# Second modulation product of a diffusion step: one 2 MB weight transfer and one buffer per group

## The chip, the cores and the metric

The kernel runs on one core of one Trainium2 chip. The metric is device time in microseconds, smaller is better. The kernel before takes 1057.17 us (median of 3 runs, 1056.76 to 1060.57).

## What is computed

One layer of a hybrid diffusion backbone, for 512 latent and 128 context tokens (640 rows of 1024 features), all in float32. Cut to the part that matters here:

```python
shift1, scale1, gate1, shift2, scale2, gate2 = jnp.split(silu(c) @ w_ada + b_ada, 6)   # for c and for c_ctx
h   = rmsnorm(x, pre1) * (1 + scale1) + shift1
mix = (g_a * y_mlstm + g_b * y_attn) @ w_out          # two mixers that both read h; g = sigmoid of h @ w_in
x   = x + gate1 * rmsnorm(mix, post1)
h   = rmsnorm(x, pre2) * (1 + scale2) + shift2
x   = x + gate2 * rmsnorm(square(relu(h @ w_mlp1)) @ w_mlp2, post2)
```

`w_ada` is 1024 x 6144. The product with it has two rows only (the latent condition `c` and the context condition `c_ctx`). Its first 2048 columns (shift1, scale1) are needed at the start; the other 4096 (scale2, shift2, gate1, gate2) are the "second modulation product", and the change is there.

## The kernel before

Large products run on TensorE in three matmuls each, on a high and a low part of the operands: `mm3` (L115) issues them on L116, L117 and L118, and names like `wh`/`wl`, `h1h`/`h1l` are such pairs. Weights reach SBUF as `raw` by SyncE's DMA queue (`load_w`, L103); ScalarE casts the high part (L111), VectorE subtracts for the low part (L112). `raw` has two buffers, and three pairs of `wh`/`wl` go round as a ring.

The stage around the change is the merge of the two mixers, from 352 to 553 us of the span. A loop over eight column blocks `j` does, for each: a product for the gate of the first mixer (48 matmuls of 320 columns), one with that mixer's output (24), the same two for the second mixer (48 and 24), then sigmoid, multiply and add on ScalarE and VectorE (L805, L808, L810) and the split of the sum into `zh`, `zl` (L811, L812). The next stage, the product with `w_out`, reads `zh` and `zl`.

The second modulation product is spread over this loop. It is a generator, `ada_rest` (L737), with eight groups `cb` of 512 columns; one step is taken ahead of the loop (L795) and one at the end of each turn (L813). A group

- loads its weights, 1024 x 512 floats or 2 MB, from GpSimd's DMA queue: four transfers of 512 KB, two k-blocks each, into a tile `aw2` with two buffers (L741, L742; the profile writes `aw` for it, as for the tile of the first product);
- multiplies in `ada_rows` (L144): eight float32 matmuls of 512 columns (L149), one per k-block. Each has a stationary operand of 32 columns (`csil`, the two conditions padded with zeros) and is put on one of four strips of the array, 32 columns wide, by `tile_position`: k-blocks 0 to 3 on strips 0 to 3, then 4 to 7 on the same strips again, added up there. In the profile each float32 matmul counts as two instructions;
- copies the result from PSUM (L150, ScalarE, tile `ar`), turns it by four transposes on TensorE (L155), adds the strips and the bias on VectorE (L157, L158), and writes it to `modA`, `modB` or `gcol`; every second of the last four groups also sends a gate to DRAM (L759 to L762).

The first product (w_ada1, in `features`, L198) uses the same `ada_rows`, with 256 columns and its weights in one 1 MB transfer per feature block from SyncE's queue.

The program is put in order by a scheduler that works from modelled times (`schedule_with_timeline_sim`): each engine runs its own list strictly in that order, and waits on semaphores. With two buffers for four transfers, the third and the fourth pair of matmuls of a group can only run after the first and second buffers have been read and filled again, so the scheduler puts them further down TensorE's list.

Of the kernel before, what the change touches and what calls it, by code (L numbers as in the profile page):

```python
# [6 lines left out]
F32 = mybir.dt.float32  # L7
# [5 lines left out]
P = 128  # L13
NT = 5
TOK = 640
KD = 8
# [10 lines left out]
def _build(ctx, tc, nc, a, dbg):  # L27
    V, S, G, T = nc.vector, nc.scalar, nc.gpsimd, nc.tensor
# [46 lines left out]
    def bank1():  # L75
        return psum[1][1].tile([P, 512], F32, name="b1")
# [67 lines left out]
    def ada_rows(raws, n, rows):  # L144

        ps = bank1()
        for k in range(KD):
            j = k % 4
            T.matmul(ps[32 * j:32 * j + 32, 0:n], csil[:, k, :], raws[k], start=k < 4, stop=k >= 4, tile_position=(0, 32 * j))  # L149
        S.copy(rows, ps[:, 0:n])  # L150

    def ada_cols(rows, nb, pt, cb, name):

        for fb in range(nb):
            T.transpose(pt[:, fb, :], rows[:, fb * 128:(fb + 1) * 128], ident)  # L155
        m = small.tile([P, 4, 2], F32, name="mc" + name)[:, 0:nb, :]
        V.tensor_reduce(out=m, in_=pt.rearrange("p b (j x) -> p b x j", j=4)[:, :, 0:2, :], axis=AX.X, op=ALU.add)  # L157
        V.tensor_tensor(out=m, in0=m, in1=b_ada[:, cb:cb + nb].unsqueeze(2).broadcast_to([P, nb, 2]), op=ALU.add)  # L158
        return m
# [89 lines left out]
    with pool("pM", side="right") as pM:  # L249
# [68 lines left out]
        for s in (4, 0, 1, 2, 3):  # L318
            c = slice(s * 128, (s + 1) * 128)
            V.tensor_tensor_scan(out=mt[:, c], data0=ar[:, c], data1=ar[:, c], initial=mc[:, s:s + 1], op0=ALU.max, op1=ALU.max)  # L320
            if s != 3:
                d = 5 if s == 4 else s + 1
# [17 lines left out]
        for (dst, src) in ((Rr, R), (srr, sr)):  # L340
            n = dst.shape[0]
# [394 lines left out]

    def ada_rest(pY):  # L737
        for cb in range(8):
            raws = []
            for u in range(4):  # L740
                raw = pY.tile([P, 2, 512], F32, name="aw2", bufs=2)  # L741
                G.dma_start(raw, a["w_ada2"][cb * 4 + u].rearrange("p (k n) -> p k n", k=2))  # L742
                raws += [raw[:, 0, :], raw[:, 1, :]]
            rows = pY.tile([P, 512], F32, name="ar2", bufs=1)
            ada_rows(raws, 512, rows)
            m = ada_cols(rows, 4, bank1().rearrange("p (b x) -> p b x", b=4), 16 + cb * 4, "2")
            kk = slice((cb % 2) * 4, (cb % 2) * 4 + 4)
            if cb < 2:
                V.scalar_tensor_tensor(out=modA[1][:, kk, :], in0=m, scalar=1.0, in1=pre2[:, kk].unsqueeze(2).broadcast_to([P, 4, 2]),
                                       op0=ALU.add, op1=ALU.mult)  # L750
            elif cb < 4:
                V.tensor_copy(modB[1][:, kk, :], m)
            else:
                g = (cb - 4) // 2
                V.tensor_tensor(out=gcol[g][:, :, kk].rearrange("p r k -> p k r"), in0=m,
                                in1=post[:, g, kk].unsqueeze(2).broadcast_to([P, 4, 2]), op=ALU.mult)
                if cb % 2:
                    pg = bank1()
                    T.transpose(pg[0:16, 0:128], gcol[g].rearrange("p r k -> p (r k)"), ident)  # L759
                    gr = pY.tile([16, 128], F32, name="gr", bufs=1)  # L760
                    V.tensor_copy(gr, pg[0:16, 0:128])
                    G.dma_start(a["scratch_gate"][g].rearrange("r (k f) -> (r k) f", f=128), gr)  # L762
            yield
# [6 lines left out]
    with pool("pY", side="right") as pY:  # L770
        ys = []
        ada = ada_rest(pY)
        for name in ("m", "a"):
            yh = pY.tile([P, 4, TOK], F32R, name="yh" + name)
# [263 lines left out]
    def u_pair():  # L1038
        return [[pF_.tile([P, TOK], F32R, name="u" + s, bufs=4) for n in range(2)] for s in "hl"]

    for ch in range(NCH):
# [25 lines left out]
        else:  # L1067
# [9 lines left out]
            for p in range(2):  # L1077
                n = ch * 2 + p
# [4 lines left out]
                u = u_pair()  # L1083
# [34 lines left out]
        for j, (t, nh, i, lo, hi) in enumerate(todo):  # L1118
            d = slice(nh * 512 + lo, nh * 512 + hi)
# [15 lines left out]
            if last and hi == 512 and nh:  # L1135
                r = small.tile([P, 1], F32, name="rs_y")
                G.tensor_tensor(out=r, in0=ms, in1=mhalf[:, 0:1], op=ALU.pow)
                for h in range(2):
                    d = slice(h * 512, h * 512 + 512)
# [14 lines left out]
def _piece_b(w):  # L1154
    import numpy as np
    kk, n = w.shape[0] // 128, w.shape[1] // 128
    return np.ascontiguousarray(w.reshape(kk, 128, n, 128).transpose(2, 1, 0, 3).reshape(n, 128, kk * 128))


def _piece_a(w, k, n):  # L1160
    import numpy as np
    nk, nn = w.shape[0] // (128 * k), w.shape[1] // n
    return np.ascontiguousarray(w.reshape(nk, k, 128, nn, n).transpose(3, 0, 2, 1, 4).reshape(nn * nk, 128, k * n))


def prepare(i):
    import numpy as np
    c_ = np.ascontiguousarray
    cols = lambda v: c_(v.reshape(-1, 128).T)
    d = {}  # L1170
    d["x"] = c_(np.concatenate([i["x_sample"][0], i["x_prompt"][0]], 0).reshape(5, 128, 1024))
    d["cache_ckv"] = c_(i["cache_mla_ckv"][0, 0])
    d["cache_krope"] = c_(i["cache_mla_krope"][0, 0])
    cn = i["state_mlstm_C"][0, 0].transpose(0, 2, 1, 3)
    nn = i["state_mlstm_n"][0, 0].transpose(0, 2, 1)[..., None]
    d["state"] = c_(np.concatenate([cn, nn], -1))
    cv = np.stack([i["c_ctx"], i["c"][0]], -1)
    cv = cv.reshape(8, 128, 2).transpose(1, 0, 2).reshape(128, 16)
    wa = i["w_ada"][0].reshape(1024, 6, 8, 128)
    d["w_ada1"] = _piece_a(wa[:, [1, 0]].transpose(0, 2, 1, 3).reshape(1024, 2048), 8, 256)  # L1180
    d["w_ada2"] = _piece_a(wa[:, [4, 3, 2, 5]].reshape(1024, 4096), 2, 512)
    b = i["b_ada"][0].reshape(6, 8, 128)
    b = np.concatenate([b[[1, 0]].transpose(1, 0, 2).reshape(16, 128), b[[4, 3, 2, 5]].reshape(32, 128)], 0).reshape(-1)
    d["vecs"] = c_(np.concatenate([cols(i["norm_pre1"][0]), cols(i["norm_pre2"][0]), c_(i["mlstm_head_norm"][0].T), cols(b),
                                   cols(i["norm_post1"][0]), cols(i["norm_post2"][0]), cv], 1))
    gb = i["mlstm_gate_b"][0]
    d["hvec"] = c_(np.stack([gb[:, 0].reshape(8), gb[:, 1].reshape(8), i["state_mlstm_m"][0, 0].reshape(8)], 1))
    d["kv_norm"], d["q_norm"] = c_(i["mla_kv_norm"][0]), c_(i["mla_q_norm"][0])
    w = i["w_in"][0]
    d["w_q"], d["w_k"] = _piece_b(w[:, 0:512]), _piece_b(w[:, 512:1024])  # L1190
    d["w_v"], d["w_o"] = _piece_a(w[:, 1024:1536], 2, 512), _piece_b(w[:, 1536:2048])
    d["w_p1"] = _piece_a(np.concatenate([w[:, 2048:2064], w[:, 2448:2704], w[:, 2704:2736]], 1), 2, 304)
    d["w_cq"] = _piece_a(w[:, 2064:2448], 2, 384)
    d["w_g"] = _piece_b(w[:, 2736:4784])
    d["w_uq"] = _piece_a(i["w_uq"][0].reshape(384, 768), 1, 768)
    ukv = i["w_ukv"][0]
    d["w_uk"] = c_(_piece_b(ukv[:, :, 0:64].reshape(256, 512)).transpose(1, 0, 2).reshape(128, 1024))
    d["w_uv"] = _piece_a(ukv[:, :, 64:128].reshape(256, 512), 2, 512)[0]
    d["w_y"] = c_(np.concatenate([_piece_b(i["w_mlstm_o"][0]), _piece_b(i["w_mla_o"][0])], 2))
    d["w_out"] = _piece_a(i["w_out"][0], 2, 512)  # L1200
    d["w_mlp1"] = _piece_b(i["w_mlp1"][0])
    d["w_mlp2"] = c_(i["w_mlp2"][0].reshape(8, 2, 2, 128, 2, 512).transpose(0, 4, 1, 3, 2, 5).reshape(8, 2, 2, 128, 1024))
    d = {k: c_(np.asarray(v)) for k, v in d.items()}

    f = np.float32
    eye = np.eye(128, dtype=f)
    s, t = np.arange(128)[:, None], np.arange(128)[None, :]
    pen_f = np.where(t >= s, 0.0, BIG).astype(f)
    pen_b = np.where(t <= s, 0.0, BIG).astype(f)
    inv = (f(10000.0) ** (-np.arange(0, 16, 2, dtype=f) / f(16))).astype(f)  # L1210
    pos = np.arange(512)
    ang = np.concatenate([(pos // 64).astype(f)[:, None] * inv, (pos % 64).astype(f)[:, None] * inv], -1)
    tab = lambda x: x.astype(f).reshape(4, 128, 16).transpose(1, 0, 2).reshape(128, 64)
    d["consts"] = c_(np.concatenate([eye, eye[::-1], pen_f, pen_b, tab(np.cos(ang)), tab(np.sin(ang))], 1))
    keep = np.ones((8, 640), f)
    keep[:, ::128] = 0.0
    d["keep"] = keep
    return d
# [28 lines left out]
```

## Time and profile before

| | |
|---|---|
| median of 3 runs | 1057.17 us (1056.76 to 1060.57) |
| the profiled execution | 1055.42 us, of which 1053.7 us is the span from first to last instruction |
| mean granted TensorE clock | 0.996 of full |
| TensorE busy | 1022.7 us, 97% of the span |
| VectorE, ScalarE, GpSimd busy | 53%, 40%, 23% |
| bytes moved by DMA | 112.03 MB, 106 GB/s on average |

The span is what the profile's rows add up to; 1.7 us lie around it. The profiled execution is 1.75 us below the median of the runs. Busy times on TensorE are of pipelined matmuls, whose ends are modelled, so the steps from one start to the next say more than the durations.

### The profile page before, as it was taken

To read this page: it belongs to the slowest core of one execution; us is meant where nothing else is said; L and a number is where in the kernel's file an instruction comes from. 1 tells how busy PE (TensorE), PEld (TensorE's weight loads), DVE (VectorE), ACT (ScalarE), POOL (GpSimd) and SP (SyncE) were. 2 spreads that over 40 slices of the span, in tenths; PEclk is the share of its full clock that TensorE was granted. 3 is DMA by queue.
4 is the path that set the end of the run, shared out by engine and by line. 5 is a ranking of instruction groups with operands and counts; after the bars stand their busy time and mean duration, and the time that the engine had idled before them with its cause. 6 is when DMAs were issued, how large, how long until landed. Compare 5 with 4: busy or idle time off the path is not lost.

```text
span 1053.7 us, 15728 instructions
## 1 busy us (share of the span) xinstructions
PE 1022.7 (97%) x6342; PEld 907.0 (86%) x6342; DVE 561.0 (53%) x955; ACT 424.2 (40%) x784; POOL 238.1 (23%) x218
## 2 busy tenths in 40 slices
PE   4999999899999999999999998999999999999997
PEld 2899899888889888888888897898989898989896
DVE  4655255767664222222334489365566565656557
ACT  4354244277775222222223564442425152515142
POOL 3011225424560000001000015224040404040101
PEclk9999999999999999999999999999999999999999
DMA  9444132211002444444446251231313131313034
GB/s 372 168 129 145 46 109 73 75 41 41 15 8 79 139 143 140 141 140 141 140 141 223 77 180 62 79 121 40 120 40 120 40 120 41 121 41 121 1 111 169
DMA packets 40121, 112.03 MB, mean 106 GB/s; under 512 B 4280, under 2 KB 14168, under 8 KB 38768
## 3 DMA queue, kind: packets, MB, share of 16 engines
q1 hardware_dynamic: 34656, 92.92, 25.8%
q0 software_dynamic: 4672, 16.80, 4.9%
q10 hardware_dynamic: 720, 1.31, 0.3%
q8 instruction: 50, 0.82, 0.3%
q14 instruction: 23, 0.19, 0.1%
HBM read 105.03 MB, written 5.98 MB: 105 GB/s over the span
## 4 chain that ended last, share of the span: by engine, by line
PE 89%; DVE 5%; ACT 2%; issue 2%; DMA 1%; POOL 1%; SPq 0%; POOLq 0%; DVEq 0%; ACTq 0%
PE b L116 20%; PE b L117 20%; PE b L118 20%; PE b L937 7%; PE bY L937 5%; PE b L149 3%; PE bV L937 2%; PE bW L937 2%; PE b L695 2%; PE b L683 2%; PE b L229 1%; PE b L496 1%; PE b L470 1%; DMA x<-x 1%; DMA gate<-w_mlp 1%
## 5 line engine op out<-in xcount | busy, mean ns | idle before, releaser
L112 DVE TENSOR_TENSOR wl<-raw,wh 128x1024 fp32r<-128x1024 f32 (+2 forms) x67 | 80.5, 1202 | 157.7 <-ACT wh L111 156.4
L111 ACT CAST wh<-raw 128x1024 fp32r<-128x1024 f32 (+2 forms) x69 | 69.8, 1013 | 175.0 <-PE b L117 157.0
L117 PE MATMUL b<-h1l,wh 128*128 128x320 f32 x400 | 125.2, 313 | 0.0
L116 PE MATMUL b<-h1h,wh 128*128 128x320 f32 x384 | 119.9, 312 | 0.0
L118 PE MATMUL b<-h1h,wl 128*128 128x320 f32 x384 | 118.9, 310 | 0.0
L117 PEld LDWEIGHTS b<-h1l,wh 128*128 128x128 f32 x400 | 75.2, 188 | 6.9 <-issue 6.9
L116 PEld LDWEIGHTS b<-h1h,wh 128*128 128x128 f32 x384 | 72.2, 188 | 7.1 <-DVE sg L808 5.0
L845 POOL TENSOR_TENSOR x<-gate 128x512 f32<-128x512 f32 x14 | 19.7, 1406 | 235.2 <-DMA gate<-w_mlp 220.8
L118 PEld LDWEIGHTS b<-h1h,wl 128*128 128x128 f32 x384 | 72.2, 188 | 0.3 <-issue 0.2
L117 PE MATMUL b<-wlx,uh 128*128 128x512 f32 (+1 forms) x164 | 64.5, 393 | 2.4 <-DVE wlx L112 2.4
L116 PE MATMUL b<-whx,uh 128*128 128x512 f32 (+1 forms) x164 | 64.1, 395 | 1.6 <-ACT u L995 1.6
L1125 DVE TENSOR_TENSOR h1h<-h1h,b 128x512 f32<-128x512 f32 (+1 forms) x71 | 46.2, 673 | 35.8 <-PE b L118 35.6
L117 PE MATMUL b<-wl,uh 128*128 128x512 f32 x160 | 63.2, 395 | 0.0
L116 PE MATMUL b<-wh,uh 128*128 128x512 f32 x160 | 62.1, 396 | 0.0
L118 PE MATMUL b<-whx,ul 128*128 128x512 f32 (+1 forms) x164 | 61.5, 393 | 0.0
L118 PE MATMUL b<-wh,ul 128*128 128x512 f32 x160 | 60.4, 394 | 0.0
L742 POOL DMA_DIRECT2D aw<-w_ada x32 | 17.4, 545 | 185.8 <-PE b L149 178.6
L999 ACT CAST uh<-u 128x320 fp32r<-128x320 f32 x64 | 29.3, 459 | 74.4 <-DVE u L996 48.7
L612 POOL TENSOR_TENSOR pt<-pt,sm 128x640 f32<-128x640 f32 x32 | 40.0, 1255 | 46.7 <-DVE sm L610 44.5
L112 DVE TENSOR_TENSOR wlx<-raw,whx 128x1024 fp32r<-128x1024 f32 (+2 forms) x28 | 34.6, 1234 | 27.9 <-ACT whx L111 27.8
L149 PE MATMUL b<-aw,csil 128*32 128x256 f32 (+1 forms) x256 | 35.2, 519 | 6.4 <-DMA aw<-w_ada 6.4
L117 PEld LDWEIGHTS b<-wlx,uh 128*128 128x128 f32 x164 | 31.1, 190 | 9.6 <-DVE wlx L112 2.8
(432 smaller groups left out, 2812.8 us busy)
## 6 DMA issues: line engine op xcount, KB each, us to landing
raw<-w_mlp SPq DMA_DIRECT2D x36, 512.0 KB, 3.2
aw<-w_ada POOLq DMA_DIRECT2D x32, 512.0 KB, 4.2
gate<-w_mlp SPq DMA_DIRECT2D x28, 512.0 KB
aw<-w_ada SPq DMA_DIRECT2D x8, 1024.0 KB, 12.0
raw<-w_g SPq DMA_DIRECT2D x16, 512.0 KB, 5.3
x<-x SPq DMA_DIRECT2D x10, 512.0 KB, 8.0
raw<-w_y SPq DMA_DIRECT2D x8, 512.0 KB, 3.3
raw<-w_out SPq DMA_DIRECT2D x8, 512.0 KB, 4.3
```

What stands on the lines that cost most here:

```text
L111: S.copy(hi, raw)
L112: eng.tensor_tensor(out=lo, in0=raw, in1=hi, op=ALU.subtract)
L116: T.matmul(out, lh, rh, start=start, stop=False)
L117: T.matmul(out, lh, rl, start=False, stop=False)
L118: T.matmul(out, ll, rh, start=False, stop=stop)
L149: T.matmul(ps[32 * j:32 * j + 32, 0:n], csil[:, k, :], raws[k], start=k < 4, stop=k >= 4, tile_position=(0, 32 * j))
L612: G.tensor_tensor(out=pt, in0=pt, in1=sm.broadcast_to([P, 640]), op=ALU.mult)
L683: T.transpose(pp[:, j * 128:(j + 1) * 128], pt[:, j * 128:(j + 1) * 128], ident)
L695: T.matmul(pv[64 * e:64 * e + 64, 0:128], vn[:, j, h * 64:(h + 1) * 64], pT[:, j, e * 128:e * 128 + 128], start=j == 0, stop=j == 4, tile_ ...
L937: T.matmul(out, w[u][:, k, :], x[v][:, k, :], start=start and k == 0 and i == 0, stop=k == 3 and i == 2, skip_group_check=True)
L999: S.copy(uh[:, c], u)
L1125: V.tensor_tensor(out=o, in0=o, in1=ps, op=ALU.add)
```

## The change

The weights of a group come in one transfer of 2 MB, 16 KB a partition, into one tile of that size, without a second buffer (`aw2` now has the pool's one buffer). The host side lays `w_ada2` out accordingly, eight k-blocks side by side instead of two. The matmuls, their operands and everything behind them stay as they are.

```diff
     def ada_rest(pY):
         for cb in range(8):
-            raws = []
-            for u in range(4):
-                raw = pY.tile([P, 2, 512], F32, name="aw2", bufs=2)
-                G.dma_start(raw, a["w_ada2"][cb * 4 + u].rearrange("p (k n) -> p k n", k=2))
-                raws += [raw[:, 0, :], raw[:, 1, :]]
+            raw = pY.tile([P, KD, 512], F32, name="aw2")
+            G.dma_start(raw, a["w_ada2"][cb].rearrange("p (k n) -> p k n", k=KD))
+            raws = [raw[:, k, :] for k in range(KD)]
             rows = pY.tile([P, 512], F32, name="ar2", bufs=1)
             ada_rows(raws, 512, rows)
...
-    d["w_ada2"] = _piece_a(wa[:, [4, 3, 2, 5]].reshape(1024, 4096), 2, 512)
+    d["w_ada2"] = _piece_a(wa[:, [4, 3, 2, 5]].reshape(1024, 4096), 8, 512)
```

From L740 on, line numbers of the changed kernel are smaller by two.

TensorE's list, where the first group begins (`b_` are PSUM tiles, `aw_` the weights of the group, and the row with L149 stands for as many matmuls as its x says). Before:

```order
L118 MATMUL b_3760<-h1h,wl_3757 128x320
L149 MATMUL b_3833<-aw_3824,csil 32x512 x2
L149 MATMUL b_3833<-aw_3826,csil 32x512 x2
L116 MATMUL b_3864<-h1h,wh_3860 128x320
L117 MATMUL b_3864<-h1l,wh_3860 128x320
```

and 43 matmuls further down the third pair of the same group:

```order
L116 MATMUL b_3864<-h1h,wh_3860 128x320
L149 MATMUL b_3833<-aw_3828,csil 32x512 x2
L117 MATMUL b_3864<-h1l,wh_3860 128x320
L118 MATMUL b_3864<-h1h,wl_3861 128x320
```

Now:

```order
L118 MATMUL b_3760<-h1h,wl_3757 128x320
L149 MATMUL b_3827<-aw_3824,csil 32x512 x8
L116 MATMUL b_3858<-h1h,wh_3854 128x320
L117 MATMUL b_3858<-h1l,wh_3854 128x320
```

Each group stood in three pieces (two pairs together, then a pair, then a pair) and stands in one, at the place where the first piece stood. The four transposes on L155, which stood in the second gate product, now follow the piece by 24 to 33 matmuls, inside the first one. All other matmuls keep their order.

ScalarE's list around the second group's copy from PSUM (`ar_`). Before:

```order
L811 CAST zh<-sg_3913 128x640
L111 CAST wh_4266<-raw 128x1024
L805 ACTIVATE sg_4116<-b_4067 128x640
L150 COPY ar_4035<-b_4036 128x512
L111 CAST wh_4349<-raw 128x1024
L805 ACTIVATE sg_4199<-b_4150 128x640
```

Now:

```order
L809 CAST zh<-sg_3907 128x640
L150 COPY ar_4023<-b_4024 128x512
L803 ACTIVATE sg_4104<-b_4055 128x640
L111 CAST wh_4248<-raw 128x1024
L111 CAST wh_4331<-raw 128x1024
L803 ACTIVATE sg_4187<-b_4138 128x640
```

The copy has moved ahead of the sigmoid, and the cast of a weight block (wh_4266, now wh_4248) behind it. VectorE's three small operations on the group move up in the same way. SyncE's list is unchanged.

GpSimd's list at the start of the stage. Before:

```order
L742 DMA aw_3824<-w_ada 128x1024
L742 DMA aw_3826<-w_ada 128x1024
L742 DMA aw_3828<-w_ada 128x1024
L742 DMA aw_3830<-w_ada 128x1024
L742 DMA aw_4027<-w_ada 128x1024
```

Now:

```order
L740 DMA aw_3824<-w_ada 128x4096
L740 DMA aw_4021<-w_ada 128x4096
L740 DMA aw_4218<-w_ada 128x4096
```

Eight issues stand where 32 stood, one for each group; from the second on each waits for the matmuls of the group before, which read the same buffer.

## Rows read from the trace of the kernel before

**Rows 1.** The page, part 1: busy time of each engine.

```profile
PE 1022.7 (97%) x6342; PEld 907.0 (86%) x6342; DVE 561.0 (53%) x955; ACT 424.2 (40%) x784; POOL 238.1 (23%) x218
```

**Rows 2.** The page, part 4: the chain that ended last, by engine.

```profile
PE 89%; DVE 5%; ACT 2%; issue 2%; DMA 1%; POOL 1%; SPq 0%; POOLq 0%; DVEq 0%; ACTq 0%
```

**Rows 3.** Windows, one per group: length; busy us; granted clock, DMA share, GB/s.

```profile
352.50:377.60 25.10, 25.10 (x166) 22.02 (x164) 6.59 (x9) 6.27 (x8) 2.14 (x4) 1.00 0.37 127
...
528.30:553.40 25.10, 25.10 (x167) 22.06 (x166) 10.05 (x13) 7.55 (x9) 1.56 (x3) 1.00 0.43 147
```

**Rows 4.** Timeline, 352.2 to 353.8: start, us, engine, line; a piece of four matmuls.

```profile
352.19 0.31 PE L117 MATMUL b<-h1l,wh 128*128 128x320 f32 x1
...
352.34 0.31 PE L118 MATMUL b<-h1h,wl 128*128 128x320 f32 x1
...
352.58 0.16 PEld L149 LDWEIGHTS b<-aw,csil 128*32 128x32 f32 x8 [0.19 <-issue]
352.58 1.06 PE L149 MATMUL b<-aw,csil 128*32 128x512 f32 x8
...
353.57 0.19 PEld L116 LDWEIGHTS b<-h1h,wh 128*128 128x128 f32 x1 [0.84 <-ACT wh L111]
353.58 0.41 PE L116 MATMUL b<-h1h,wh 128*128 128x320 f32 x1
...
353.83 0.31 PE L117 MATMUL b<-h1l,wh 128*128 128x320 f32 x1
```

**Rows 5.** Timeline of TensorE, 363.3 to 364.9: a piece of two matmuls.

```profile
363.37 0.31 PE L117 MATMUL b<-ylm,wh 128*128 128x320 f32 x1
363.61 1.05 PE L149 MATMUL b<-aw,csil 128*32 128x512 f32 x4
364.60 0.41 PE L118 MATMUL b<-yhm,wl 128*128 128x320 f32 x1
364.85 0.30 PE L116 MATMUL b<-yhm,wh 128*128 128x320 f32 x1
```

**Rows 6.** Timeline, 27.6 to 28.7: eight matmuls of 256 columns (first product).

```profile
27.67 1.07 PE L149 MATMUL b<-aw,csil 128*32 128x256 f32 x16
28.67 0.33 PE L211 MATMUL b<-cst,x 128*128 128x128 f32 x1
```

**Rows 7.** Groups by shape, two windows: busy us, mean ns of one | idle before.

```profile
L149 PE MATMUL b<-aw,csil 128*32 128x512 f32 x128 | 25.4, 605 | 0.0
...
L149 PE MATMUL b<-aw,csil 128*32 128x256 f32 x16 | 1.1, 385 | 0.0
```

**Rows 8.** Timeline of GpSimd's queue, 324 to 356: issues, idle before them.

```profile
353.94 1.07 POOL L742 DMA_DIRECT2D aw<-w_ada  x2 [27.19 <-PE b L149]
```

**Rows 9.** The tile `aw`, 320 to 560: us from issue to landing.

```profile
DMA to landing us min/median/max: 3.6/4.2/6.1
```

**Rows 10.** DMA, 325 to 550: the queue's packets, MB and share of 16 engines.

```profile
q0 software_dynamic: 4660, 16.79, 22.7%
```

**Rows 11.** The page, part 6: the first product's loads, KB each, us to landing.

```profile
aw<-w_ada SPq DMA_DIRECT2D x8, 1024.0 KB, 12.0
```

**Rows 12.** Timeline of ScalarE, 402.5 to 428.5; L149's piece starts at 402.80.

```profile
404.69 0.73 ACT L811 CAST zh<-sg 128x640 fp32r<-128x640 f32 x1 [0.89 <-DVE sg L810]
412.21 1.05 ACT L111 CAST wh<-raw 128x1024 fp32r<-128x1024 f32 x1 [6.80 <-PE b L117]
...
413.76 0.58 ACT L150 COPY ar<-b 128x512 f32<-128x512 f32 x1
```

**Rows 13.** Timeline of ScalarE, 549 to 561: casts of the next stage's weights.

```profile
553.55 1.05 ACT L111 CAST wh<-raw 128x1024 fp32r<-128x1024 f32 x1 [1.82 <-PE b L117]
...
559.97 1.05 ACT L111 CAST whx<-raw 128x1024 fp32r<-128x1024 f32 x1 [2.81 <-DMA raw<-w_out]
```

**Rows 14.** Timeline of TensorE at 649; then the windows view of 650.2 to 653.6.

```profile
649.20 0.50 PE L117 MATMUL b<-wlx,uh 128*128 128x512 f32 x1 [2.37 <-DVE wlx L112]
...
650.20:653.60 3.40, 3.28 (x8) 1.99 (x6) 3.40 (x7) 2.38 (x4) 0.00 (x0) 0.50 0.72 220
```

## The prediction

> **What bounds the kernel now.** I read the page's busy times first: TensorE is busy 97% of the span, the next engine 53% [rows 1]. The chain that ended last says the same from the other side, 89% of it is TensorE [rows 2]. Then I cut the stage of the change into eight windows, one from each group's first modulation matmul to the next one's: in the first and the last, as in the six between, TensorE is busy for the whole 25.10 us at full clock, while VectorE and ScalarE are busy 6 to 10 us, GpSimd about 2, and the DMA engines 0.37 and 0.43 of the time [rows 3]. So here nothing waits in TensorE's place. A microsecond taken off its list in this stage comes off the end, as long as what feeds it keeps up; and no saving elsewhere in the stage is worth anything.
>
> **What a piece costs before.** The unit is the step from start to start, since durations overlap. Three-part matmuls of 320 columns step by 0.15 us (352.19 to 352.34) [rows 4]. Around a piece of four modulation matmuls the matmul before starts at 352.34 and the second one after it at 353.83: 1.49 us where two plain steps would be 0.30, so the piece costs 1.19 us [rows 4]. Around a piece of two it is 363.37 to 364.85, 1.48 us, again 1.19 [rows 5]. Four matmuls cost what two cost: those on different strips of the array run side by side, and the price is one of pieces. Part of it is the change of shape itself: the first full-width weight load behind a piece starts 0.84 us after the loads before it ended [rows 4]. A group has three pieces, eight groups have 24: 24 x 1.19 = 28.6 us on the path.
>
> **What it costs after.** A group is one piece of eight, two matmuls deep on each strip. The trace of before has no such piece with 512 columns, but it has one with 256: it runs from 27.67 to 28.67, 1.00 us, just like the piece of four with 512 (352.58 to 353.58) [rows 4, 6]. Both push 512 columns through each strip. The time per pass follows: each float32 matmul is two instructions, so four matmuls are two rounds; the piece is busy 1.06 us and its last instruction takes 0.605 us, so the second round starts 0.455 us after the first [rows 4, 7]. With 256 columns there are four rounds: (1.07 - 0.385) / 3 = 0.23 us each [rows 6, 7], half as much. The four starts within a round are a little staggered, which is in both figures, so I take 0.44 us a round. Eight matmuls of 512 columns add two rounds, 0.88 us: 1.19 + 0.88 = 2.07 us a piece, 8 x 2.07 = 16.6 us in all. The gain is 28.6 - 16.6 = **12.0 us**. Bounds: at worst the second four cost as much as a piece of their own, 2.38 us, and the gain is 28.6 - 19.0 = 9.6 us; at best a round is 0.42 us and it is 12.3.
>
> The rows show what lets rounds follow closely: the eight weight loads of a piece are through 0.16 us after its start, while its matmuls run for 1.06 us [rows 4]. The Trainium skill, page "TensorE: Matmul & The Clock Gate", Part 3 ("The mechanism"), says that a weight load overlaps with matmuls in flight only if it is for another group of rows; all these loads use the same 128 rows. By that rule each of the two added rounds would wait for its loads first, at most 0.16 us [rows 4] each time, and the gain would be 12.0 - 8 x 2 x 0.16 = 9.4 us; the row here disagrees with it, and I follow the row.
>
> **What moves at no cost, and its cover.** ScalarE's copy of the result (L150, 0.58 us) now stands right behind the split L811 [rows 12]. That one ended 2.6 us after the piece's start (404.69 + 0.73 against 402.80), the piece itself ends after about 1.9, so the copy is done near 3.3 us; the transposes that need it come 24 or more steps behind the piece, at 2.1 + 24 x 0.15 = 5.7 us. That is 2.4 us of cover; without it TensorE would wait. Behind the copy stand the sigmoid, which waits for the 48 matmuls of its product anyway, and a weight cast 0.7 us later than before, for a block that is used a whole turn later. VectorE's three small operations wait for the transposes in both versions, and the next operation behind them there waits for that cast. The transposes cost TensorE the same four steps as before. GpSimd loses 24 issues of 0.54 us [rows 8], on an engine that idles.
>
> **What is added: a wait for 2 MB into a single buffer.** Before, a transfer filled one buffer while the other was read. Now it is issued when the piece has ended, some 2.2 us after its start (before: 353.94 against 352.58, 1.36 us, plus 0.88) [rows 4, 8], and must land before the next group's piece. A group's turn shrinks from 25.1 [rows 3] to 23.6 us, so 21.4 us are left. How long does it take? 16.79 MB of this queue filled 22.7% of 16 engines over 225 us, that is 51 us of all engines, or 6.4 us for 2.1 MB [rows 10]. A 512 KB transfer would then take 1.6 us of moving; it lands in 4.2 [rows 9], so 2.6 us are fixed: 9.0 us for 2 MB. A weight transfer of 512 KB that shares the engines adds up to 1.6. Lower bound 9.0; upper bounds are two of the first product's 1 MB loads in a row, 2 x 12.0 = 24.0 [rows 11], and four of the slowest 512 KB ones in a row, 4 x 6.1 = 24.4 [rows 9]. I take 10 us: those 12.0 were measured at the start, with many other loads in flight, and the rows nearest in queue, bytes and place are the lower ones. The wait is then hidden, with 11 us to spare. The first load has longer: the queue had issued its first two and stood idle for 27.19 us before 353.94 [rows 8]. The burst can hold up the merge's own weight loads by at most its 6.4 us; the casts that use them sit idle for TensorE [rows 12], and the blocks are used a turn later, so I price that at zero; without that cover it would be those 6.4 us a turn.
>
> **Sum.** Against the profiled execution: 1055.4 - 12.0 = 1043.4 us. The median of the runs was 1.75 us above that execution, so for a median I forecast **1045.2 us**, 1.1% less. About 0.5%, 5.3 us here, is what a measurement of this kernel can tell from no change.
>
> **Rivals.**
>
> 1. *The single buffer becomes the bound (slower).* TensorE would stand at the head of each piece until 2 MB have landed, seven times. The price is 7 x (L - 21.4) for a landing time L: the gain is gone at L = 21.4 + 12.0 / 7 = 23.1 us, and at the upper bound of 24.4 us it is 7 x 3.0 = 21 us against 12, so 1057.2 + 9 = 1066 us. For it speak rows 11; against it that the DMA engines are busy only some 0.4 of the time in this stage [rows 3] and that rows 9 and 10 give less than half of that L. The Trainium skill, page "Trainium Kernel Development and Optimization", section "Best Practices", asks to double-buffer so that transfers overlap with compute, and this change gives that up; by the rule this rival would win, and the trace so far bears it out only if L passes 21.4 us. Chance 0.05.
>
> 2. *The next stage takes half of it back.* Its weights arrive late already: the cast at 559.97 waited 2.81 us for DMA [rows 13]. If those loads kept their old times, TensorE would meet them early and wait. Against it: the cast ahead of them, at 553.55, waited for TensorE [rows 13], and the loads wait in turn for buffers that such casts free, so the whole chain should move up with TensorE. Half lost is 1051.2 us. Chance 0.09.
>
> 3. *It doesn't do what it says.* If the second four matmuls waited for something that the 256-column piece doesn't show, and cost all that the separate pieces did, the time stays at 1057. Rows 6 speak against that. Chance 0.04.
>
> **How the numbers follow.** The forecast has 0.82. Its own range: gain 9.6 to 12.3 us, and one stretch of 3.4 us in which the clock fell to half (0.50, the 1.2 GHz level) after TensorE had waited 2.37 us [rows 14]; it costs some 1.7 us and may come or go. With the spread of the runs that is 1041 to 1048. The range I give goes on to rival 2, **1040.5 to 1052**; outside are rivals 1 and 3 and the far part of 2. Faster by over 0.5%: 0.86 (the forecast and half of rival 2); within 0.5%: 0.09 (the other half and rival 3); slower: 0.05 (rival 1).
>
> **What would show it.** In the profile after: eight pieces of 16 instructions on L149, each about 2.07 us by the step measure; windows of 23.6 us with TensorE busy throughout; loads of 2 MB that land 9 to 11 us after issue; no wait of TensorE for `aw` or for `ar`; the rest as long as before. It is wrong if TensorE waits at the head of pieces (rival 1), at 540 to 555 us (rival 2), or if a piece takes over 2.4 us (rival 3).

## The result, and the profile after

| | before | after |
|---|---|---|
| median (6 runs each) | 1057.61 us (1055.65 to 1061.43) | **1047.03 us** (1046.60 to 1047.85) |
| ratio, 95% interval | | 0.9894 (0.9875 to 0.9914) |
| profiled execution | 1055.42 us, span 1053.7 | 1047.85 us, span 1046.1 |

The kernel is 1.1% faster. The page of the kernel after: busy times (part 1), the chain that ended last (part 4), the loads' issues on GpSimd (part 5: busy us, mean ns | idle before) and the transfers (part 6: KB each, median us to landing).

```profile
PE 1013.2 (97%) x6342; PEld 909.4 (87%) x6342; DVE 558.9 (53%) x955; ACT 425.2 (41%) x784; POOL 225.3 (22%) x194
...
PE 89%; DVE 4%; ACT 2%; DMA 2%; issue 2%; POOL 1%; SPq 0%; POOLq 0%; DVEq 0%; ACTq 0%
...
L740 POOL DMA_DIRECT2D aw<-w_ada x8 | 4.5, 569 | 165.6 <-PE b L149 158.3
...
aw<-w_ada POOLq DMA_DIRECT2D x8, 2048.0 KB, 8.8
```

TensorE has the same 6342 matmuls and is 9.5 us less busy than in [rows 1]; its share of the chain is unchanged [rows 2]. Eight issues have taken the place of 32, and each 2 MB lands in 8.8 us. (From here on the line numbers after the load are two lower than before.)

The windows view, first and last group of the kernel after, in the columns of [rows 3]:

```profile
355.59:379.20 23.61, 23.61 (x166) 21.97 (x165) 6.59 (x9) 6.27 (x9) 0.54 (x1) 1.00 0.36 136
...
520.91:544.51 23.60, 23.60 (x166) 22.10 (x166) 9.97 (x13) 7.52 (x9) 0.50 (x1) 1.00 0.35 113
```

A turn is 23.6 us where it was 25.1, TensorE is busy for all of it, and the clock is full. So the wait for the single buffer, which the prediction had to bound, isn't there. The timeline of one piece, with the weight loads (PEld) that go with it:

```profile
402.41 0.31 PE L117 MATMUL b<-yla,wh 128*128 128x320 f32 x1
...
402.56 0.31 PE L118 MATMUL b<-yha,wl 128*128 128x320 f32 x1
...
402.80 0.16 PEld L149 LDWEIGHTS b<-aw,csil 128*32 128x32 f32 x8 [0.19 <-issue]
402.80 1.92 PE L149 MATMUL b<-aw,csil 128*32 128x512 f32 x16
...
403.25 0.13 PEld L149 LDWEIGHTS b<-aw,csil 128*32 128x32 f32 x4 [0.30 <-issue]
403.68 0.13 PEld L149 LDWEIGHTS b<-aw,csil 128*32 128x32 f32 x4 [0.30 <-issue]
...
404.65 0.42 PE L116 MATMUL b<-h1h,wh 128*128 128x320 f32 x1
...
404.90 0.31 PE L117 MATMUL b<-h1l,wh 128*128 128x320 f32 x1
```

By the measure of the prediction: from the matmul before the piece to the second one behind it, 402.56 to 404.90, are 2.34 us, less two plain steps of 0.15: a piece costs 2.04 us. Over the eight pieces, instruction by instruction and with a plain step of 0.147 us, it is 2.05 each, 16.42 us in all; the same count on the kernel before gives 8 x 1.191 + 16 x 1.180 = 28.41 us. The difference is 11.99 us.

Yet the two profiled spans differ by 7.6 us only, and the medians by 10.6. To see where the rest went, cut each span in three: up to the first piece, from there to the first matmul that reads `zh` or `zl` (the stage), and from there to the end. All profiles of this study, in microseconds:

| profile | time | up to the stage | the stage | behind it |
|---|---|---|---|---|
| before | 1055.42 | 352.58 | 200.91 | 500.17 |
| before, again | 1058.82 | 354.50 | 200.92 | 501.64 |
| after | 1047.85 | 355.59 | 188.96 | 501.53 |
| after, again | 1046.22 | 353.81 | 188.95 | 501.64 |
| four buffers | 1048.39 | 355.08 | 188.95 | 502.59 |
| two pieces | 1048.70 | 353.51 | 191.69 | 501.73 |
| three pieces | 1059.71 | 355.27 | 200.95 | 501.72 |
| load twice | 1047.45 | 356.30 | 188.94 | 500.43 |
| load three times | 1065.65 | 355.30 | 185.67, one piece short | 522.91 |
| three times, first five | 1047.39 | 355.28 | 188.81 | 501.54 |

In the first pair 11.95 us come from the stage; 3.01 are lost ahead of it and 1.36 behind it, in parts of the program that the diff doesn't touch. In the second pair the stage gives 11.97, and the other two parts 0.69 and 0.00. For one and the same kernel the stage repeats to 0.01 us; over all profiles the column ahead of it spreads over 3.7 us and the one behind it over 2.4 (without the load issued three times).

### The profile page after: what moved, and what is told of

The parts are those of the page before. It is cut to its first block, busy times and chain, and to the rows that moved or that the text cites. A ratio compares the mean times of both kernels' runs of the same rounds, so it can differ in the third digit from the quotient of the medians.

```text
span 1046.1 us, 15677 instructions
## 1 busy us (share of the span) xinstructions
PE 1013.2 (97%) x6342; PEld 909.4 (87%) x6342; DVE 558.9 (53%) x955; ACT 425.2 (41%) x784; POOL 225.3 (22%) x194
## 4 chain that ended last, share of the span: by engine, by line
PE 89%; DVE 4%; ACT 2%; DMA 2%; issue 2%; POOL 1%; SPq 0%; POOLq 0%; DVEq 0%; ACTq 0%
PE b L116 20%; PE b L118 20%; PE b L117 20%; PE b L935 7%; PE bY L935 5%; PE bV L935 2%; PE bW L935 2%; PE b L149 2%; PE b L695 2%; PE b L229 2%; PE b L683 1%; PE b L470 1%; PE b L472 1%; DMA x<-x 1%; PE b L496 1%
## 5 line engine op out<-in xcount | busy, mean ns | idle before, releaser
L740 POOL DMA_DIRECT2D aw<-w_ada x8 | 4.5, 569 | 165.6 <-PE b L149 158.3
L116 PEld LDWEIGHTS b<-whx,uh 128*128 128x128 f32 x164 | 30.8, 189 | 10.4 <-ACT u L993 3.6
```

Source lines behind the costliest of these rows:

```text
L116: T.matmul(out, lh, rh, start=start, stop=False)
```

## Experiments

The theory: **the price is one of pieces** on TensorE's list, 1.19 us for each that is one matmul deep on a strip and 2.05 for one that is two deep; the number of transfers and the single buffer don't matter as long as the weights land within the 21.4 us from one piece to the next. The rivals: the gain comes from fewer and longer transfers; the single buffer is close to its bound; what was lost outside the stage belongs to the change.

### The pieces or the transfers

**Four buffers.** The transfers of the kernel before, the pieces of the kernel after. Edit, against the kernel before:

```diff
-                raw = pY.tile([P, 2, 512], F32, name="aw2", bufs=2)
+                raw = pY.tile([P, 2, 512], F32, name="aw2", bufs=4)
```

Expected:

> The four 512 KB transfers of the kernel before, into four buffers instead of two; the eight matmuls then stand in one piece. Theory (the price is of pieces): eight pieces of 2.05 us, 16.4 us in the stage, and the time of the changed kernel within 1 us, about 1047 us. Rival (the gain comes from fewer and longer transfers): 24 issues as before, so the time of the kernel before, about 1057 us; between the two if both count.

Measured: 1047.63 us (1046.80 to 1049.04), ratio to before 0.9913 (0.9899 to 0.9927). The windows view of TensorE over the whole stage (length, busy, instructions, granted clock, DMA share, GB/s):

```profile
355.08:544.03 188.95, 188.95 (x1315) 1.00 0.41 148
```

The timeline shows one piece to a group, here the third:

```profile
402.29 1.92 PE L149 MATMUL b<-aw,csil 128*32 128x512 f32 x16
```

The stage is as long as that of the kernel after, with 32 transfers of 512 KB, and its eight pieces come to 16.42 us as well. The size of the transfer gives nothing by itself. The whole time is 1.5 us above that of the kernel after in the same comparison (1046.15 us, below), with intervals of the ratio that overlap; in the profile the parts outside the stage are what differs.

**Three pieces.** The other corner: the transfer of the kernel after, the pieces of the kernel before, in about their old places. Edit, against the kernel after:

```diff
-            ada_rows(raws, 512, rows)
+            ps = bank1()
+            for k in range(KD):
+                if k in (4, 6):
+                    yield
+                j = k % 4
+                T.matmul(ps[32 * j:32 * j + 32, 0:512], csil[:, k, :], raws[k], start=k < 4, stop=k >= 4, tile_position=(0, 32 * j))
+            S.copy(rows, ps[:, 0:512])
...
                 mode_b(pg, w, h1, KD)
+                if q == 0:
+                    next(ada, None)
...
                 sgs.append(sg)
+                if q == 0:
+                    next(ada, None)
```

Expected:

> The changed kernel, one 2 MB transfer a group, with its eight matmuls in three pieces of 4, 2 and 2, in about the places that they have in the kernel before. Theory: 24 pieces of 1.19 us are 28.6 us in the stage, all of the gain is gone, and the time is that of the kernel before within 1.5 us, about 1057 us; the single buffer has some 12 us from the end of the last piece to the next group's first, enough for a landing of 9 us. Rival (transfers): the time of the changed kernel, 1047 us. If the landing passes those 12 us, TensorE waits at the head of the first piece and the time is above 1058 us.

Measured: 1057.73 us (1055.34 to 1059.81), ratio 1.0003 (0.9992 to 1.0014). The stage, in the same view:

```profile
355.27:556.22 200.95, 200.95 (x1316) 1.00 0.40 140
```

One transfer of 2 MB, 24 pieces (28.4 us in all), and the whole gain is gone: the stage is back to 200.95 us against 200.91. All eight k-blocks lie in SBUF at once here too, and that alone gives nothing either: it is what lets the eight matmuls stand in one piece, and the piece brings the gain. The single buffer still doesn't show, although some 12 us of its slack of 21.4 are left.

**Two pieces.** Between the two: `if k == 4` in place of `if k in (4, 6)`, and only the first of the two added `next` calls. Expected:

> The changed kernel, one 2 MB transfer a group, with its eight matmuls in two pieces of four, one third of a turn apart. Theory: 16 pieces of 1.19 us are 19.0 us in the stage where eight of 2.05 us are 16.4, so 2.6 us slower than the changed kernel, about 1049.6 us. Rival (the second four cost nothing extra wherever they stand, or the transfers make the gain): the time of the changed kernel. Rival (the transformation is worth as much again as from three to two pieces, 12 us for 16 pieces less, 0.75 us each): 6 us slower, 1053 us.

Measured: 1048.43 us (1047.86 to 1048.70), ratio 0.9918 (0.9904 to 0.9931), 2.3 us above the kernel after in the same comparison. The stage, and the timeline of a second piece (L748 is where its matmuls stand in this kernel):

```profile
353.51:545.20 191.69, 191.69 (x1316) 1.00 0.41 146
```

```profile
361.51 0.31 PE L118 MATMUL b<-h1h,wl 128*128 128x320 f32 x1
361.75 1.07 PE L748 MATMUL b<-aw,csil 128*32 128x512 f32 x8
362.74 0.41 PE L116 MATMUL b<-yhm,wh 128*128 128x320 f32 x1
362.99 0.31 PE L117 MATMUL b<-ylm,wh 128*128 128x320 f32 x1
```

361.51 to 362.99 is 1.48 us, less two steps 1.18; all 16 pieces come to 19.09 us, where 16.42 stood. The stage is 2.74 us longer. So the saving is not even: from three pieces to two it is 9.3 us, since a piece of 2 costs as much as one of 4; from two to one 2.7, since the second four matmuls still need their two rounds.

### What lay outside the stage

Nothing is edited here; both kernels were profiled a second time. Expected:

> The changed kernel once more, for a second profile. Theory: the stage gives 12.0 us and what lay outside it in the first pair of profiles (TensorE 3.0 us further behind by 199 us, with a half-clock stretch of 3.41 us at 196 us, and 1.2 us more around 650 us) varies from run to run; then this profile lacks the stretch at 196 us, or a second profile of the kernel before shows one too, and the median lies 10 to 12.5 us below the kernel before. Rival: the loss outside the stage belongs to the change; then the same stretch stands at 196 us again, with the same 3 us, and the median lies no more than 10.6 us below.

> The kernel before, for a second profile. Four profiles with other stages behind it show TensorE at the stage's start 0.7 to 3.4 us later than the first profile of before, most of it from a stall and a half-clock stretch at 194 to 200 us, although nothing ahead of the stage is changed. Theory (this varies from run to run, and the first profile was a quick one: 1055.4 us where the median is 1057.9): the second profile lies near 1057 to 1058 us, and its stretch at 194 to 200 us looks like that of the others, 1 to 3 us later than in the first. Rival (the larger buffer or the shorter program shifts something upstream): again 1055.4 us and no half-clock stretch there.

Measured, after: 1046.15 us (1045.33 to 1047.05), ratio 0.9898 (0.9884 to 0.9911), 11.8 us below before. Before again: 1057.50 us (1055.65 to 1058.89) against 1057.97, ratio 0.9993 (0.9980 to 1.0005). The windows view of TensorE from 193 to 203 us, where the first pair had parted, first of the first profile of before, then of its second, then of the kernel after:

```profile
193.00:203.00 10.00, 8.51 (x59) 1.00 0.18 54
```

```profile
193.00:203.00 10.00, 9.10 (x49) 0.66 0.17 54
```

```profile
193.00:203.00 10.00, 7.20 (x43) 0.83 0.17 52
```

The granted clock falls to the lower level for part of this stretch in the second profile of the same kernel, more than in the kernel after, and fewer matmuls get through (49 against 59). So the rival that the stretch belongs to the change falls: the kernel before has it too. Of the ten profiles two show full clock here (the first of before, and two pieces), five show 0.83 and three 0.66. The first profile of before was one of the quick ones.

### How much the single buffer stands

**Load twice, load three times.** Each load is issued so many times into the same buffer; each issue waits for the landing of the one before it. Edit, against the kernel after:

```diff
-            G.dma_start(raw, a["w_ada2"][cb].rearrange("p (k n) -> p k n", k=KD))
+            for _ in range(3):
+                G.dma_start(raw, a["w_ada2"][cb].rearrange("p (k n) -> p k n", k=KD))
```

Expected:

> The changed kernel with each 2 MB load issued twice into the same buffer, the second when the first has landed; nothing else is changed. Theory (the landing is hidden as long as it is under the 21.4 us from the piece's end to the next piece): the weights are there some 2 x 8.8 = 17.6 us after the first issue, TensorE waits nowhere, and the time is that of the changed kernel within 1.5 us, about 1047 us. Rival (the single buffer is near to its bound, or the traffic holds up the merge's own weights): 3 us slower or more.

> The changed kernel with each 2 MB load issued three times into the same buffer, one after the other. Theory: the weights are there 3 x 8.8 = 26.4 us after the first issue, 5.0 us past the 21.4 us, and TensorE waits at the head of seven pieces: 7 x 5.0 = 35 us slower than the changed kernel, about 1082 us, somewhat more where the clock falls during the waits. Rival (the cover is longer than 21.4 us, as the piece's start could be put off): less than 20 us slower.

Measured, twice: 1047.23 us (1045.63 to 1048.34), ratio 0.9900 (0.9882 to 0.9918), as expected. GpSimd's timeline (issue, and the idle time before it) and the stage:

```profile
382.59 0.54 POOL L741 DMA_DIRECT2D aw<-w_ada  x1 [14.69 <-PE b L149]
393.38 0.54 POOL L741 DMA_DIRECT2D aw<-w_ada  x1 [10.25 <-DMA aw<-w_ada]
405.75 0.54 POOL L741 DMA_DIRECT2D aw<-w_ada  x1 [11.83 <-PE b L149]
```

```profile
356.30:545.24 188.94, 188.94 (x1315) 1.00 0.61 226
```

The second issue stands 10.8 us behind the first, so the weights are there some 20 us after it (10.8 and a landing of 8.9), near the 21.4 that there are; the DMA engines are busy 0.61 of the stage instead of 0.41; nothing is lost. The pieces stand where they stood but for three places: 161 to 167 instructions of TensorE from one to the next, where the kernel after has 164 or 165.

Three times: 1065.70 us (1065.23 to 1067.65), ratio 1.0079 (1.0061 to 1.0097). That is 19 us above the kernel after, and not 35. The windows view of TensorE over the stage, and its timeline at the last two pieces:

```profile
355.30:540.97 185.67, 185.67 (x1289) 1.00 0.73 275
```

```profile
539.12 1.92 PE L149 MATMUL b<-aw,csil 128*32 128x512 f32 x16
...
566.68 3.64 PE L149 MATMUL b<-aw,csil 128*32 128x512 f32 x16 [11.01 <-DMA aw<-w_ada]
571.07 1.11 PE L155 MATMUL b<-cst,ar 128*128 128x128 f32 x4 [0.75 <-ACT ar L150]
```

TensorE waits at none of the first seven pieces: it is busy for all of the 185.67 us. In this kernel's program they stand further apart (387.41, 418.20, 447.80, 477.71: some 30 us instead of 23.6), with other matmuls between them: 205 to 222 instructions from one piece to the next instead of 164 or 165. The list of this kernel is another one, with each piece put later; that the scheduler did so because its modelled times include the longer load is the plain reading, and not shown. Only the eighth had no merge work left to stand behind. It stands behind some 60 matmuls of the next stage, waited 11.01 us all the same, and TensorE ran the piece at the lower clock, in 3.64 us instead of 1.92.

The 11 us are not all of the 19. The windows view of TensorE from the first to the last matmul that reads `zh` or `zl`, first of the kernel after, then of this one:

```profile
544.55:602.98 58.43, 58.43 (x266) 1.00 0.45 161
```

```profile
540.97:622.11 81.14, 66.51 (x292) 0.87 0.52 194
```

This stretch is 22.7 us longer, of which 3.3 only moved here from the stage (188.95 less 185.67: the eighth piece and some transposes). Of the other 19.4 us, 14.6 are idle time, the 11.0 at the piece and 3.6 in shorter waits behind it, and the remaining 4.8 go with the lower granted clock (0.87 over the stretch).

**Three times in the first five groups.** If only the end pays, late loads early in the stage must be free. Edit: `range(3 if cb < 5 else 1)`. Expected:

> As with the load issued three times, but in the first five groups alone; the last three load once. With three loads in all eight groups the turn grew to 30 us, yet TensorE did not wait at the pieces: the planner that orders the program had put them some 200 instead of 146 steps apart, other matmuls filled the time, and only the last piece, with no merge work left behind it, waited 11.0 us. Theory (a load that is late is paid for at the end of the stage alone): the last three pieces catch up, the eighth stands where it stands in the changed kernel, no piece waits, and the time is that of the changed kernel within 1.5 us, about 1047 us, with a stage of 189 us. Rival (each late group costs its share of the 18.7 us, 2.7 us for each of seven): some 4 x 2.7 = 11 us slower, 1058 us.

Measured: 1047.52 us (1045.35 to 1050.07), ratio 0.9902 (0.9883 to 0.9921). The stage:

```profile
355.28:544.09 188.81, 188.81 (x1314) 1.00 0.64 237
```

Five groups load three times, the pieces start 32, 31, 30 and 30 us apart, the last three catch up (490.74, 505.08, 520.46), and the stage is no longer than that of the kernel after. TensorE waits for none of the late loads within it; the first piece waited 0.4 us, just ahead of it. The rival, 2.7 us for each late group, falls.

Two plain alternatives were not tried: a second buffer of 2 MB, and one piece made of two groups.

## Why the prediction was right

- **What a piece costs before** (24 x 1.19 = 28.6 us): 28.41 measured; the pieces of two cost 1.18 us, which is also what [rows 5] give. That its price doesn't depend on whether it holds 2 or 4 matmuls was the basis of the sum, and the kernels with two and three pieces bear it out.
- **What it costs after** (2.07 us, from rounds of 0.44 us that were taken from a piece of the first product, half as wide): 2.05 us. The four rounds start at 0, 0.453, 0.882 and 1.311 us. So a piece costs some 0.33 us beside its rounds at either depth (1.19 less two rounds of 0.43, 2.05 less four). The 0.84 us between weight loads that the prediction read as the change of shape [rows 4] are something else: they stand behind pieces of either depth, and for most of them the last two rounds are running. The gain in the stage, 12.0 us forecast, is 11.95 and 11.97 us in the two pairs of profiles; so rival 3, that the second four would cost all that separate pieces did, fell. In the timeline above the weights of the third round are loaded at 403.25, those of the fourth at 403.68, each while the round before it runs. The Trainium skill, page "TensorE: Matmul & The Clock Gate", Part 3 ("The mechanism"), lets a weight load overlap with running matmuls, in its list of what overlaps, only if it is for another group of rows, though its text above the list also names a background weight buffer; all of these are for the same 128 rows. By the rule of the list the gain was 9.4 us; this trace disagrees with it.
- **ScalarE's copy** (done 3.3 us after the piece's start, where its terms add up to 3.2; 2.4 us of cover). The timeline of the kernel after, for the piece at 402.80:

```profile
405.32 0.58 ACT L150 COPY ar<-b 128x512 f32<-128x512 f32 x1
...
408.87 0.60 PE L155 MATMUL b<-cst,ar 128*128 128x128 f32 x4
```

The copy ends at 405.90, 3.1 us after the start; the transposes start 3.0 us later, and wait for nothing.

- **The wait for 2 MB** (10 us, bounds 9.0 and 24.4): the loads land in 8.8 us, 8.3 to 10.2. The lower bound was a little too high. It took the moving time from the queue's share of the engines, 22.7% [rows 10]; the same bytes in fewer packets took less. The DMA view from 325 to 550 us of the kernel after:

```profile
q0 software_dynamic: 1216, 16.79, 20.1%
```

That is 5.7 us a load instead of 6.4. Nothing hung on the error, with 21.4 us to land in. The traffic held up none of the merge's own weights on the path: TensorE is busy for all of the stage, with two loads a group as well.

- **Rival 1**, the single buffer as the bound, didn't come; at 8.8 us against 21.4 it was far off. But **its price was wrong**. The prediction made TensorE wait "seven times", 7 x (L - 21.4). With three loads L is about 28 us (issues at 389.66, 399.62 and 409.42, then 8.5), which by that formula is some 46 to 48 us; 19 were lost. The step that failed there is that the list stays as it is: in the kernel that was built the pieces stand further apart, and only the last, with no work of its own stage left to stand behind, waits.
- **Rival 2**, the next stage giving half back, didn't come. The product with `w_out` takes TensorE 58.43 us after, as shown above, and the same 58.43 before (553.49 to 611.92), without a wait in either. The whole part behind the stage is 501.5 and 501.6 us after, 500.2 and 501.6 before.
- **The sum.** 1045.2 us was forecast, 1047.03 measured: 1.8 us more, within the range. No term of the change explains it, as each on TensorE's list came out within 0.2 us. 0.4 us are the base, 1057.17 us in three runs and 1057.61 in six. The other 1.4 us are within the noise: the interval of the ratio, 0.9875 to 0.9914, is a gain of 9.1 to 13.2 us. Over all the comparisons the median of before was 1057.6 to 1058.4 us, and the ten runs of the kernel after have a median of 1046.6; the two differ by 11 to 12 us. The prediction allowed 1.7 us for one half-clock stretch that may come or go; the parts outside the stage spread by 3.7 and 2.4 us. Whether the change moves them by some tenths of a microsecond can't be told from these runs.

## What to carry to other kernels

Where matmuls of another shape are put into a stream, count the interruptions, not the matmuls: here 2 or 4 of them, side by side on the strips, cost the same 1.19 us, and 8 in one piece cost 2.05. The gain came from one piece in place of three, and having all operands in SBUF at once, however they got there, is what allowed it. A single buffer is enough where the landing time is under the time from one use to the next: here 8.8 us, and even some 20, against 21.4. Before pricing a late transfer as a wait at each use, ask what the scheduler can put in front of it; here only the last use of the stage, with no work of the stage left, had to wait.

## What was not expected of the hardware

Rounds on the four strips follow one another with no gap that the rows show, at either clock. At full clock they start 0.429 us apart, and the second 0.453 us after the first; in the piece of 256 columns [rows 6] the same steps are 0.215 and 0.240 us. Half the columns take half the time, so next to nothing of a round is a fixed wait for its weights. At the lower level the rounds start 0.853 us apart, the second 0.826 after the first, as in the last piece of the kernel that loads three times. Its windows view from 566.6 to 570.6, with TensorE's busy time, weight loads and granted clock:

```profile
566.60:570.60 4.00, 3.64 (x16) 0.68 (x16) 0.00 (x0) 0.17 (x1) 0.00 (x0) 0.50 0.02 4
```

The 16 weight loads take 0.68 us there, nearly all of it while the matmuls run.

And a wait of about the same length may be followed by the lower clock or not. At 194 us TensorE waits for VectorE in every profile. The timeline there and the windows view, first of the kernel with two pieces, then of the one with three loads in five groups:

```profile
194.62 0.46 PE L470 MATMUL b<-va,wt 128*128 128x129 f32 x2 [3.14 <-DVE C L500]
```

```profile
193.00:203.00 10.00, 7.78 (x55) 1.00 0.18 54
```

```profile
195.00 0.77 PE L470 MATMUL b<-va,wt 128*128 128x129 f32 x2 [2.29 <-DVE C L500]
```

```profile
193.00:203.00 10.00, 7.94 (x48) 0.83 0.19 54
```

The longer wait has full clock behind it, the shorter one has not. As two profiles of one kernel differ here as well (those of before), the half-clock stretch at 194 us is a term of the spread in these runs, and not of the change.
